# Two tags for the raw pieces at the changes of operands, and another order of PSUM banks in the plain groups of a gated MLP

## The chip, the cores and the metric

One core of a Trainium2 chip runs the whole kernel. The metric is the device time of one execution in microseconds; a kernel's time is the median of its runs. The engines are named as in the profile: PE (TensorE), ACT (ScalarE), DVE (VectorE), POOL (GpSimd) and SP (SyncE), whose instruction queue issues every DMA of this kernel.

## The reference

One decoder layer over 2048 tokens of width 1024: a mixer of three head groups with an output projection, then a gated MLP with a causal width-3 convolution on its gate branch, then a last norm. The change touches only the MLP's second half; the mixer is left out here.

```python
h = rmsnorm(x, norm_ffn[l])                                  # (2048, 1024)
gate = causal_dwconv(h @ ffn_w_gate[l], ffn_conv_w[l], ffn_conv_b[l])   # (2048, 2688)
x = x + (jax.nn.gelu(gate) * (h @ ffn_w_val[l])) @ ffn_w_down[l]        # 2688 -> 1024
...
return rmsnorm(x, norm_final)
```

## The kernel before

Matrix products run in a split float format: each operand is kept as a high and a low part (`split`, line 110: ACT copies the high part, DVE subtracts it from the raw tile for the low one), and each product takes three matmuls (`mm3`, line 134; the loop at line 1067). The large products of the MLP are 2x2 block products computed with seven block products in place of eight (`seven`, line 1062); the moving operand of such a product is held as four sets of tiles, `b1`, `t12`, `t34` and `b22` (`new_H`, line 895), which are the blocks and their sums. One `seven` is 84 matmuls of 128x512 and accumulates in one PSUM bank of tag `mm` (four banks), one of `sc` (two) and one of `aux` (two), asked for in that order.

The MLP is seven stages, in program order (lines 1251 to 1279):

- `up(0)`, for tokens 0 to 1023: 21 blocks `f` of 128 columns of the gate and value weights, one `seven` each. Its products are written to DRAM (`gx_d`, `gr_d`). Beside it `h_next` writes the operand tiles of the second token half, raw, to `hb_d`.
- `plain([(0, 4)])`: the first 5 of the 21 rows of `w_down` (NX = 5) as ordinary products, for 4 token tiles. Beside it `h_load` reads the raw operand pieces from `hb_d` and splits them into the operand tiles of `up(1)`: 14 pieces of 128x1024, three after each `f`.
- `up(1)`: tokens 1024 to 2047.
- `plain([(4, 4), (8, 2)])`: 4 and then 2 token tiles. Beside it `d_steps(0, H)` makes the operand tiles of `down(0)` out of 8 rows of `w_down`: four steps of two raw tiles of 128x1024, one after each of the first four `f`.
- `down(0)`: 8 rows of `w_down` for all tokens, 8 pairs of token tiles, one `seven` each.
- `plain([(10, 3), (13, 3)])`, beside it `d_steps(1, H)`; then `down(1)`, which also takes the last norm and writes the output.

These three `plain` stages are the changes of operands: while PE works through plain products, ACT and DVE make the next set of operand tiles. Below they are called the first, second and third change.

In `plain` (line 1146) each `f` loads a raw row of `w_down` (`load_w`, tag `wr` of pool `wraw`, three buffers; its parts `wh` and `wl` have three buffers, pool `wsp`) and a piece `graw` of the products (two buffers), splits both, and multiplies for every token tile `t` and both column halves `h`. The last two `f` are held back and run at the end, tile by tile; then ACT copies the two banks of `t` into a tile `y` (pool `op`, four buffers), which is stored to `ps_d`. With `n` token tiles one `f` is 6n matmuls.

What the raw tiles share:

- `wr`, three buffers: the raw weights of `plain` (`load_w`), those of `d_steps` (line 1002), and the raw weights of the stage that follows (`a_steps`, line 1031).
- `xt` of pool `xpool`, two buffers: the 14 pieces of `h_load` (line 991), and the sums `s12` and `s34` that `a_steps` makes for each `seven` (lines 1047 and 1053).
- `y`, four buffers in each change: the copied banks (line 1176), and in `down` the tiles that take the sums (line 1195). Its pool is opened where the tiles `gr`, `ga` and `v` of the `up` stage before were, so in the first and second change a `y` is free once those tiles of the last block are.

The banks of a group before:

```python
banks = [[aux_bank(), sc_bank()] if t < 2 else [mm_bank(), mm_bank()] for t in range(n)]
```

Each engine runs its own queue in order. The order within a queue is laid out when the kernel is built, by a planner that takes instructions by program order and by the offsets of `tc.high_priority`, and that gives out buffers as it expects them to come free; the splits of `plain` stand under such offsets (320 for the weights, 160 for `graw`), the copies of the banks do not.

Of the kernel before, what the change touches and what calls it, by code (L numbers as in the profile page):

```python
# [44 lines left out]
def kernel(ctx: ExitStack, tc: tile.TileContext, x, norm_mix, w_in, hgrn_lower_bounds, hgrn_norm,  # L45
# [669 lines left out]
    with ExitStack() as cy:  # L715
# [271 lines left out]

        def h_load(H):

            def piece(nm, k0):  # L990
                r = xpool.tile([P, D], F32, name="hr", tag="xt").rearrange("p (a b) -> p a b", b=TB)
                sync.dma_start(out=r, in_=hb_d[nm][:, k0:k0 + 2, :])
                put(r, H[nm], k0)
            return [lambda nm=nm, k0=k0: piece(nm, k0) for nm, n in (("t12", KT), ("b1", KT), ("b22", KH), ("t34", KT))
                    for k0 in range(0, n, 2)]

        def d_steps(r, H):

            def pair(k):
                raws = []  # L1000
                for f in (NX + KT * r + k, NX + KT * r + KH + k):
                    raws.append(wraw.tile([P, D], F32, name="wr", tag="wr"))
                    sync.dma_start(out=raws[-1], in_=w_down[f * P:(f + 1) * P, :])
# [142 lines left out]
        def plain(groups, gp, op, beside=()):  # L1146
# [3 lines left out]
            for t0, n in groups:  # L1150
                hf, at = t0 * P // TH, t0 * P % TH
                banks = [[aux_bank(), sc_bank()] if t < 2 else [mm_bank(), mm_bank()] for t in range(n)]
                ops = []
# [21 lines left out]
                for t in range(n):  # L1175
                    y = op.tile([P, D], F32, name="y", bufs=4)
                    for h in range(2):
                        for f in range(NX - 2, NX):
                            mms(t, h, f)
                        copy(act, y[:, h * 512:(h + 1) * 512], banks[t][h])  # L1180
                    sync.dma_start(out=ps_d[0][t0 + t], in_=y)
                    have[t0 + t].append(ps_d[0][t0 + t])

        def down(r, H, pairs, gp, op):
# [7 lines left out]
            def use(t0, W, steps):  # L1192
                ys = []
                for t in (t0, t0 + 1):
                    y = op.tile([P, D], F32, name="y", bufs=4)
                    sync.dma_start(out=y, in_=have[t][0])
# [63 lines left out]
        with ExitStack() as cu:  # L1260
            gp = pool_at(cu, 320, "f_g", 1, reuse_waits="tile")
            op = cu.enter_context(tc.tile_pool(name="f_o", bufs=1, reuse_waits="tile"))
            H = new_H()
            plain([(0, 4)], gp, op, h_load(H))
        with ExitStack() as cu:
# [3 lines left out]
        with ExitStack() as cu:  # L1269
            gp = pool_at(cu, 320, "f_g2", 1, reuse_waits="tile")  # L1270
            op = cu.enter_context(tc.tile_pool(name="f_o2", bufs=1, reuse_waits="tile"))
            H = new_H()
            plain([(4, 4), (8, 2)], gp, op, d_steps(0, H))
            nfb = xpool.tile([P, D], F32, name="nfb", tag="wbc", bufs=1)
            sync.dma_start(out=nfb, in_=norm_final.partition_broadcast(P))
            down(0, H, [10, 12, 14, 0, 2, 4, 6, 8], gp, op)
            H = new_H()
            plain([(10, 3), (13, 3)], gp, op, d_steps(1, H))
            down(1, H, [0, 2, 4, 6, 8, 10, 12, 14], gp, op)
# [30 lines left out]
```

## Time and profile before

| | us |
|---|---|
| median of 3 runs | 2254.43 |
| lowest and highest run | 2249.42, 2262.86 |
| the profiled execution | 2247.57 |
| its span, first to last instruction | 2245.8 |
| its time outside the span | 1.77 |

The profile is of one execution. Read it from the engine that is busiest, PE, and look for the stretches in which PE is not busy or runs at a lower granted clock; what ended the idle time is named behind the arrow of a row. A matmul's own duration in the trace is longer than the distance between the starts of two matmuls, since they are pipelined; the distance is what counts. In this document a stage's time is taken between the first matmul of the stage and the first one of the next.

### The profile page before, as it was taken

How to read it: one execution, taken by the hardware profiler on the slowest of the kernel's cores; microseconds unless marked ns; L12 is line 12 of the kernel's file. 1: busy time of each engine (PE TensorE's matmuls, PEld its weight loads, DVE VectorE, ACT ScalarE, POOL GpSimd, SP SyncE). 2: the span in 40 equal slices, each digit the busy share in tenths (PEclk: the TensorE clock that was granted, in tenths of full speed). 3: DMA queues.
4: the chain of work that ended last, by engine and by line, in shares of the span. 5: the costliest groups of instructions: out<-in, count | busy, mean ns of one | idle time of the engine just before them, and what ended most of it. 6: DMA issues, size and time to landing. Idle time of an engine off the chain costs nothing.

```text
span 2245.8 us, 31437 instructions
## 1 busy us (share of the span) xinstructions
PE 2153.5 (96%) x12118; PEld 1768.0 (79%) x12118; DVE 1679.3 (75%) x2366; ACT 990.4 (44%) x1361; POOL 353.6 (16%) x456
## 2 busy tenths in 40 slices
PE   7999999999999999999999999899999989998998
PEld 6887777777667788988888888788888867886886
DVE  7799998989678778777676766666666685777676
ACT  3443534432166276544444445444444463125332
POOL 2231332416243321000000000000000000000000
PEclk9999999999999999999999999999999999998999
DMA  7453422346145645644233337422222248646653
GB/s 261 123 165 93 154 83 64 91 159 198 38 136 207 186 152 177 205 129 129 88 123 99 125 100 231 130 85 85 85 85 85 85 166 279 223 169 223 216 181 112
DMA packets 313699, 321.41 MB, mean 143 GB/s; under 512 B 17347, under 2 KB 267214, under 8 KB 312014
## 3 DMA queue, kind: packets, MB, share of 16 engines
q1 hardware_dynamic: 313550, 319.41, 43.9%
q8 instruction: 95, 1.56, 0.3%
q14 instruction: 54, 0.44, 0.1%
HBM read 233.38 MB, written 85.98 MB: 142 GB/s over the span
## 4 chain that ended last, share of the span: by engine, by line
PE 51%; DVE 8%; DMA 6%; ACT 3%; issue 2%; POOL 0%; SPq 0%; DVEq 0%; POOLq 0%; ACTq 0%
PE mm L1068 26%; PE sc L1068 13%; PE aux L1068 6%; DMA wr<-in_ffn_w_down_dram 1%; PE sc L137 1%; DVE wl L113 1%; PE sc L136 1%; PE sc L138 1%; DMA xt<-x_d 1%; DMA y<-ps_d 1%; DMA x_d<-xr 1%; DMA hr<-hb_t 1%; ACT wh L106 1%; PE mm L913 1%; DVE xc L801 1%
## 5 line engine op out<-in xcount | busy, mean ns | idle before, releaser
L106 ACT ACTIVATE wh<-wr 128x1024 fp32r<-128x1024 f32 (+3 forms) x217 | 201.1, 929 | 362.8 <-PE aux L1068 85.0
L113 DVE TENSOR_TENSOR wl<-wr,wh 128x1024 fp32r<-128x1024 f32 (+2 forms) x241 | 261.2, 1086 | 114.8 <-ACT wh L106 110.4
L106 ACT ACTIVATE wh<-s 128x1024 fp32r<-128x1024 f32 x116 | 123.0, 1061 | 253.4 <-PE sc L1068 197.2
L138 PE MATMUL mm<-hTh,wl 128*128 128x512 f32 x576 | 230.5, 400 | 2.8 <-POOL wl L113 2.3
L136 PE MATMUL mm<-hTh,wh 128*128 128x512 f32 x576 | 232.9, 405 | 0.0
L137 PE MATMUL mm<-hTl,wh 128*128 128x512 f32 x576 | 231.0, 401 | 0.0
L404 POOL TENSOR_TENSOR qc<-Q,X 32x128 f32<-32x128 f32 x224 | 151.1, 675 | 247.1 <-ACT X L390 116.4
L1068 PE MATMUL mm<-t34h,wh 128*128 128x512 f32 x464 | 181.0, 390 | 1.1 <-DVE y L1233 0.9
L1068 PE MATMUL mm<-t34h,wl 128*128 128x512 f32 x464 | 180.6, 389 | 0.0
L1068 PE MATMUL mm<-t34l,wh 128*128 128x512 f32 x464 | 180.6, 389 | 0.0
L113 DVE TENSOR_TENSOR wl<-s,wh 128x1024 fp32r<-128x1024 f32 x116 | 141.5, 1221 | 15.0 <-ACT wh L106 14.8
L137 PE MATMUL sc<-wl,oh 128*128 128x256 f32 x512 | 147.8, 289 | 2.2 <-DVE wl L113 2.2
L136 PE MATMUL sc<-wh,oh 128*128 128x256 f32 x512 | 147.5, 289 | 2.1 <-DVE xr L834 2.1
L138 PE MATMUL sc<-wh,ol 128*128 128x256 f32 x512 | 146.3, 286 | 0.0
L138 PEld LDWEIGHTS mm<-hTh,wl 128*128 128x128 f32 x576 | 108.2, 188 | 31.3 <-issue 4.3
L136 PEld LDWEIGHTS mm<-hTh,wh 128*128 128x128 f32 x576 | 108.1, 188 | 28.8 <-issue 7.1
L137 PEld LDWEIGHTS mm<-hTl,wh 128*128 128x128 f32 x576 | 108.2, 188 | 27.8 <-issue 7.3
L1137 DVE SCALAR_TENSOR_TENSOR ga<-gr,pcol,ga 128x1024 f32<-128x1024 f32 x84 | 107.6, 1281 | 0.6 <-issue 0.3
L1068 PEld LDWEIGHTS mm<-t34h,wh 128*128 128x128 f32 x464 | 87.1, 188 | 21.2 <-issue 1.7
L137 PEld LDWEIGHTS sc<-wl,oh 128*128 128x128 f32 x512 | 98.4, 192 | 5.9 <-issue 2.9
L136 PEld LDWEIGHTS sc<-wh,oh 128*128 128x128 f32 x512 | 98.1, 192 | 5.1 <-DVE xr L834 2.7
L1068 PEld LDWEIGHTS mm<-t34h,wl 128*128 128x128 f32 x464 | 87.1, 188 | 18.2
(331 smaller groups left out, 5520.3 us busy)
## 6 DMA issues: line engine op xcount, KB each, us to landing
wr<-in_w_in_dram SPq DMA_DIRECT2D x80, 512.0 KB
wr<-in_ffn_w_gate_dram SPq DMA_DIRECT2D x42, 512.0 KB
wr<-in_ffn_w_val_dram SPq DMA_DIRECT2D x42, 512.0 KB
wr<-in_ffn_w_down_dram SPq DMA_DIRECT2D x41, 512.0 KB
wr<-in_w_out_dram SPq DMA_DIRECT2D x32, 512.0 KB
gr_d<-v SPq DMA_DIRECT2D x32, 512.0 KB
ps_d<-y SPq DMA_DIRECT2D x32, 512.0 KB
wr<-gr_d SPq DMA_DIRECT2D x32, 512.0 KB
```

What stands on the lines that cost most here:

```text
L106: act.activation(o, i, AF.Copy)
L113: e_lo.tensor_tensor(lo, raw, hi.bitcast(F32), op=ALU.subtract)
L136: pe.matmul(o, lh, rh, start=first, stop=False)
L137: pe.matmul(o, lh, rl, start=False, stop=False)
L138: pe.matmul(o, ll, rh, start=False, stop=last)
L404: pool.tensor_tensor(qc[p_, h, :].rearrange("p (n s) -> p n s", s=lev), qo[p_, 2], xo[p_, 2], op=ALU.mult)
L801: vec.tensor_tensor_scan(xc[:, i, :], r[:, i, :], th[:, i, :], initial=hs0[:, c:c + 1], op0=ALU.mult, op1=ALU.add)
L913: pe.transpose(out=pt[:, k * P:(k + 1) * P], in_=xt[:, (k0 + k) * P:(k0 + k + 1) * P], identity=ident)
L1068: pe.matmul(o, lhs[a], rhs[b], start=first and k == 0 and i == 0, stop=last and k == KH - 1 and i == 2, skip_group_check=True)
L1137: vec.scalar_tensor_tensor(ga, gr[:, k:k + TH], pc[f"fw{k}"][:, f:f + 1], ga, op0=ALU.mult, op1=ALU.add)
```

## The change

- A function `spare(op)` gives a tile of tag `y` (four buffers) or, without a pool, of tag `xt` (two buffers).
- `h_load`: the pieces of `b22` and `t34` (6 of 14) go through `y`, the others stay in `xt`.
- `d_steps`: the raw weights of steps 1 and 3 go through `y`, those of steps 0 and 2 through `xt`; none goes through `wr` any more.
- `plain`: token tile 0 and 1 take two banks of `mm` each, tile 2 the two of `sc`, tile 3 the two of `aux`; before it was `aux` and `sc` for tiles 0 and 1, `mm` for 2 and 3. The copies of the banks get a priority offset of 120.
- The tiles `y` of `plain` and `down` are the same ones as before, now written `spare(op)`.

No instruction of arithmetic and no transfer is added or taken away.

```diff
@@ -985,21 +985,25 @@
                 keep(T["t1"], "t34", KH, t)
             return [lambda f=f, t=t: f(t) for t in range(NTK) for f in (s_norm, s_a, s_b, s_c, s_d)]
 
-        def h_load(H):
+        def spare(op):
+            return op.tile([P, D], F32, name="y", tag="y", bufs=4) if op else \
+                xpool.tile([P, D], F32, name="hr", tag="xt")
+
+        def h_load(H, op):
 
             def piece(nm, k0):
-                r = xpool.tile([P, D], F32, name="hr", tag="xt").rearrange("p (a b) -> p a b", b=TB)
+                r = spare(op if nm in ("b22", "t34") else None).rearrange("p (a b) -> p a b", b=TB)
                 sync.dma_start(out=r, in_=hb_d[nm][:, k0:k0 + 2, :])
                 put(r, H[nm], k0)
             return [lambda nm=nm, k0=k0: piece(nm, k0) for nm, n in (("t12", KT), ("b1", KT), ("b22", KH), ("t34", KT))
                     for k0 in range(0, n, 2)]
 
-        def d_steps(r, H):
+        def d_steps(r, H, op):
 
             def pair(k):
                 raws = []
                 for f in (NX + KT * r + k, NX + KT * r + KH + k):
-                    raws.append(wraw.tile([P, D], F32, name="wr", tag="wr"))
+                    raws.append(spare(op if k % 2 else None))
                     sync.dma_start(out=raws[-1], in_=w_down[f * P:(f + 1) * P, :])
                 (b11, b12), (b21, b22) = [(a[:, :TB], a[:, TB:]) for a in raws]
 
@@ -1149,7 +1153,7 @@
             every = -(-len(beside) // nst)
             for t0, n in groups:
                 hf, at = t0 * P // TH, t0 * P % TH
-                banks = [[aux_bank(), sc_bank()] if t < 2 else [mm_bank(), mm_bank()] for t in range(n)]
+                banks = [[mk() for _ in range(2)] for mk in (mm_bank, mm_bank, sc_bank, aux_bank)[:n]]
                 ops = []
 
                 def mms(t, h, f):
@@ -1173,11 +1177,12 @@
                         st_()
                     cnt += 1
                 for t in range(n):
-                    y = op.tile([P, D], F32, name="y", bufs=4)
+                    y = spare(op)
                     for h in range(2):
                         for f in range(NX - 2, NX):
                             mms(t, h, f)
-                        copy(act, y[:, h * 512:(h + 1) * 512], banks[t][h])
+                        with tc.high_priority(offset=120):
+                            copy(act, y[:, h * 512:(h + 1) * 512], banks[t][h])
                     sync.dma_start(out=ps_d[0][t0 + t], in_=y)
                     have[t0 + t].append(ps_d[0][t0 + t])
 
@@ -1192,7 +1197,7 @@
             def use(t0, W, steps):
                 ys = []
                 for t in (t0, t0 + 1):
-                    y = op.tile([P, D], F32, name="y", bufs=4)
+                    y = spare(op)
                     sync.dma_start(out=y, in_=have[t][0])
                     ys.append(y)
                     for src in have[t][1:]:
@@ -1261,7 +1266,7 @@
             gp = pool_at(cu, 320, "f_g", 1, reuse_waits="tile")
             op = cu.enter_context(tc.tile_pool(name="f_o", bufs=1, reuse_waits="tile"))
             H = new_H()
-            plain([(0, 4)], gp, op, h_load(H))
+            plain([(0, 4)], gp, op, h_load(H, op))
         with ExitStack() as cu:
             upools = [pool_at(cu, 8192, "f_up1", 1, reuse_waits="tile")]
             upools.insert(0, cu.enter_context(tc.tile_pool(name="f_up0", bufs=1, reuse_waits="tile")))
@@ -1270,12 +1275,12 @@
             gp = pool_at(cu, 320, "f_g2", 1, reuse_waits="tile")
             op = cu.enter_context(tc.tile_pool(name="f_o2", bufs=1, reuse_waits="tile"))
             H = new_H()
-            plain([(4, 4), (8, 2)], gp, op, d_steps(0, H))
+            plain([(4, 4), (8, 2)], gp, op, d_steps(0, H, op))
             nfb = xpool.tile([P, D], F32, name="nfb", tag="wbc", bufs=1)
             sync.dma_start(out=nfb, in_=norm_final.partition_broadcast(P))
             down(0, H, [10, 12, 14, 0, 2, 4, 6, 8], gp, op)
             H = new_H()
-            plain([(10, 3), (13, 3)], gp, op, d_steps(1, H))
+            plain([(10, 3), (13, 3)], gp, op, d_steps(1, H, op))
             down(1, H, [0, 2, 4, 6, 8, 10, 12, 14], gp, op)
```

## Rows read from the trace of the kernel before

**Rows 1.** Page: busy time, share of the span and instructions of each engine.

```profile
PE 2153.5 (96%) x12118; PEld 1768.0 (79%) x12118; DVE 1679.3 (75%) x2366; ACT 990.4 (44%) x1361; POOL 353.6 (16%) x456
```

**Rows 2.** Windows: length, busy PE PEld DVE ACT POOL, PEclk, DMA share, GB/s.

```profile
1437.00:1817.00 380.00, 380.00 (x1678) 314.67 (x1677) 248.25 (x284) 165.81 (x206) 25.67 (x39) 1.00 0.27 86
...
1840.00:1860.00 20.00, 16.21 (x59) 12.59 (x58) 13.85 (x21) 14.07 (x23) 0.00 (x0) 0.83 0.66 241
1860.00:1880.00 20.00, 18.91 (x80) 14.51 (x80) 11.21 (x13) 8.26 (x12) 0.00 (x0) 1.00 0.93 309
2040.00:2060.00 20.00, 13.02 (x32) 9.49 (x33) 15.12 (x24) 11.26 (x19) 0.00 (x0) 0.66 0.52 169
```

**Rows 3.** Timeline of PE: start, duration, line, out<-in, idle before it.

```profile
1380.43 0.39 PE L136 MATMUL aux<-wh,gh 128*128 128x512 f32 x1
...
1436.54 0.39 PE L1068 MATMUL mm<-hTh,wh 128*128 128x512 f32 x1
...
1817.34 0.39 PE L136 MATMUL aux<-wh,gh 128*128 128x512 f32 x1
...
1838.86 0.50 PE L136 MATMUL aux<-wh,gh 128*128 128x512 f32 x1 [3.17 <-ACT wh L106]
...
1848.38 0.79 PE L136 MATMUL aux<-wh,gh 128*128 128x512 f32 x1 [3.79 <-ACT wh L106]
...
1871.98 0.39 PE L1068 MATMUL mm<-hTh,wh 128*128 128x512 f32 x1
...
2024.90 0.39 PE L136 MATMUL aux<-wh,gh 128*128 128x512 f32 x1
...
2081.64 0.39 PE L1068 MATMUL mm<-hTh,wh 128*128 128x512 f32 x1
```

**Rows 4.** Waits around the three changes in turn: total us, times, longest.

```profile
PE sc L1068 <- ACT wh L106: 3.9, 1, 3.9
...
PE mm L1068 <- ACT y L106: 1.9, 1, 1.9
...
PE aux L136 <- ACT wh L106: 9.3, 4, 3.8
...
PE aux L136 <- ACT wh L106: 7.7, 3, 3.9
...
PE mm L1068 <- DVE y L1229: 0.7, 1, 0.7
```

**Rows 5.** Chain that ended last, around the three changes: start, us, what.

```profile
1413.33 5.57 DMA hr<-hb_t
...
1833.32 4.41 DMA wr<-in_ffn_w_down_dram
...
2080.55 6.04 DMA y<-ps_d
```

**Rows 6.** Timeline of DVE in the first and the second change.

```profile
1416.80 1.23 DVE L113 TENSOR_TENSOR t34l<-hr,t34h 128x1024 fp32r<-128x1024 f32 x1 [3.50 <-ACT t34h L106]
1418.06 0.69 DVE L1048 TENSOR_TENSOR s<-wr 128x512 f32<-128x512 f32 x1
...
1822.30 1.22 DVE L1140 TENSOR_TENSOR v<-ga,v 128x1024 f32<-128x1024 f32 x1
...
1850.18 0.69 DVE L1021 TENSOR_TENSOR st<-wr,st 128x512 f32<-128x512 f32 x1
```

**Rows 7.** SP's own waits, third change: total us, times, longest.

```profile
SPq L1003 <- DVE st L1018: 9.0, 3, 3.2
...
SPq L122 <- DVE wl L113: 7.5, 3, 3.7
```

**Rows 8.** Windows over the second change, its first group, and the third change.

```profile
1807.00:1872.00 65.00, 55.63 (x228) 43.78 (x227) 51.23 (x73) 40.77 (x65) 2.25 (x1) 0.95 0.65 225
1807.00:1853.00 46.00, 37.55 (x154) 29.58 (x153) 42.22 (x62) 28.99 (x48) 2.25 (x1) 0.94 0.56 191
2014.00:2082.00 68.00, 58.92 (x231) 46.18 (x230) 49.32 (x71) 38.16 (x59) 0.00 (x0) 0.90 0.66 218
```

## The prediction

> **What bounds the kernel now.** I read the busy times first: PE is busy 96% of the span, no other engine above 79% [rows 1]. So a change that removes no arithmetic can only give back what PE loses, and the next question is where that is. The table of busy times by stretch answers it. In the long stretch of `up(1)` PE never rests: 1678 matmuls in 380.0 us, 0.2265 us from start to start, at a clock of 1.00 [rows 2]. In the stretches around the changes of operands it rests, and the granted clock falls as far as 0.83 and 0.66 on a mean over 20 us [rows 2]. [...] The fall stands behind idle times of PE in each case.
>
> The loss of each change is its length between first matmuls [rows 3] less its matmuls, counted from the code, at 0.2265 us:
> - first change with the first `seven` behind it: 1380.43 to 1436.54, 56.1 us; 5 x 24 + 84 = 204 matmuls, 46.2 us; lost 9.9.
> - second: 1817.34 to 1871.98, 54.6 us; 5 x 24 + 5 x 12 = 180, 40.8 us; lost 13.9.
> - third: 2024.90 to 2081.64, 56.7 us; 2 x 5 x 18 = 180, 40.8 us; lost 16.0, and 0.7 more just behind it, where `down(1)` waits for its first sum [rows 4].
>
> Together 40.5 us, clock losses included. What PE waited for is named by the waits and the chain. First change: 1.9 us for a bank that ACT had not yet copied, 3.9 us for the high part of `s12` [rows 4]; on the chain stand the pieces `hr`, 5.6 us each, one behind another, and `s12` itself begins right when a piece frees its `xt` buffer [rows 5, 6]. Second and third: 9.3 and 7.7 us for the high part of a plain weight [rows 4], which waited for its load, 4.4 us from issue to landing [rows 5]; two steps begin 9.5 us apart, where 24 matmuls take 5.4 [rows 3]. SP's waits say why: the loads of `d_steps` (L1003) and of `plain` (L122) both stand waiting for DVE to finish with an earlier raw tile [rows 7]. Three `wr` buffers serve three raw tiles a step.
>
> **The change part by part.** *Pieces through `y`.* 6 of the 14 pieces leave `xt`; the other 8 end with `b1`. `s12` then waits only for those, so it is made some 20 us earlier (8 pieces ahead of it, not 14, in a chain of about 60 us), and the 3.9 us with its clock loss goes. What is late next is the buffer for its parts: `wh` has three, and the two last `f` hold two of them to the end of the group. PE then has 12 matmuls of the first product, 2.7 us, in which the low part's subtraction takes 1.23 us [rows 6] and the copy before it may take as long. `down(0)` at 1871.98 begins in the same pattern, and no idle time stands before it [rows 3]. Bounds: 0 to 3.9. The `t34` pieces are needed only 48 matmuls, 10.9 us, after the start of `up(1)`.
>
> *Banks.* In the first change the first bank asked for next (`mm`) was that of tile 2; now it is tile 0's, copied 36 held-back matmuls (8 us) before the end. The 1.9 us goes. In the second change the group of two now ends on all four `mm` banks, and `down(0)` asks for one at once; tile 0's was finished 18 matmuls, 4.1 us, before, and the whole wait for such a copy is 1.9 us now [rows 4]. Nothing, unless the copy is late (rival below). I put the first change at 1.0 left of 9.9, nearer the zero end because its causes are both taken away: **8.9**.
>
> *Raw weights out of `wr`.* `plain` has the three `wr` buffers to itself and can load three rows ahead; the raw tiles of the steps have two `xt` and four `y` buffers. In the second change the first `y` buffers are free when the last `up` block has been multiplied (1822.3 to 1823.5) [rows 6], early enough for step 1. The waits for `wh` have no cause left in the loads. What is late next is DVE: it is busy 51.2 of the 65 us of the second change and 49.3 of the 68 us of the third [rows 8]. With 13.9 and 16.0 us taken out, 51.1 and 52.0 remain, so DVE would be busy nearly without a break. Over the 46 us in which the second change's steps are made its packing is 42.2 of 46, 0.918 [rows 8]. At that packing it needs 55.8 and 53.7 us: 4.7 and 1.7 too many. Of the four steps' work, four subtractions of 0.69 [rows 6] (for the `t34` parts of the last one) may come 10.9 us into `down`, which takes off some 2. Bounds 0 and 4.7; I take 2.5 and 1.7.
>
> *DMA.* The second change moves 225 GB/s over 65 us, 14.6 MB, the third 218 over 68, 14.8 MB [rows 8]. The busiest 20 us moved 309 GB/s at a share of 0.93 [rows 2]; at that rate 47.3 and 48.0 us, inside the 51.1 and 52.0 that would remain, but with little to spare. It is tight at the end of the second change, where a step of 12 matmuls lasts 2.7 us and bank stores and the loads of `down(0)` meet. If the 6.2 MB of that busiest row had all to land within the 13.6 us of the group of two, 20 - 13.6 = 6.4 us would be lost; if the earlier loads have cleared the way, nothing more than today's 0.9. I take 3.0. In the third, `y` tiles for `down(1)` took 6.0 us to land [rows 5]; I leave 1.3 for them, between 0 and 3.
> [...]
>
> Second change: 13.9 - 2.5 - 3.0 = **8.4**. Third: 16.7 - 1.7 - 1.3 = **13.7**. Sum 8.9 + 8.4 + 13.7 = 31.0 us. The profiled execution took 2247.6 us (span 2245.8, 1.8 outside), so it would be 2216.6; the median of the runs shown is 6.9 us above that execution, and from it I forecast 2254.4 - 31.0 = 2223.4 us.
>
> **The rivals.**
> - *DVE and ACT take the steps first.* With all raw tiles there early, the four steps' splits (over half of what DVE does in a change) could be laid out ahead of the plain weights; a step would stay at 9.5 us, only its releaser being another. For it: DVE at 42 of 46 us already. Against it: the plain splits stand under a priority offset of 320, the steps' under none. Gain 8.9 and some 2.5 of the second groups: 2243 us.
> - *The copies wait for raw tiles.* Copies and steps now share four `y`. The copy of tile 2 needs the buffer of step 3's first raw tile, which DVE last read at 1850.2 [rows 6]; without stalls, tile 2 is complete at 1817.3 + 27.2 - 2.7 = 1841.8. ACT would stand up to 8.4 us, with the splits of the next group behind it; 2.7 us of those are covered by the `f` already split. That is 5.7 us in the second change and about as much, 6.7, in the third, where tile 2's `sc` banks are also asked for again: 31 - 12.4 = 18.6 us, 2236 us. Against it: a planner that sees the buffer taken will put ready work first. [...]
> - *The transfers set the pace anyway.* If DMA and not the buffers is behind the 5.6 us of a piece, earlier issues land no earlier: 2254 us, no change. For it: a share of 0.93 at 1860 to 1880. Against it: only 0.66 and 0.52 in the 20 us that hold the worst stalls [rows 2].
> - *Slower: SP stands in front of a raw tile.* Place: the first groups of the second and third change. If the loads of steps 1 to 3 are queued ahead of the plain loads, SP stands until their `y` or `xt` buffer is free, and the plain loads behind it start only then. A step would then last a step's DVE work, 7 to 8 us (42.2 us for four steps, five plain splits and the tail of `up`), and then a load of 4.4 and its split, 1.2 [rows 5, 6]: 12.6 to 13.6 us in place of 9.5, so some 3.5 us lost in each of eight steps, 28, against 8.9 gained in the first change: about 2273 us. It decides from a step of 9.5 + 8.9/8 = 10.6 us. For it: SP already spends 9.0 and 7.5 us at L1003 and L122 in the third change [rows 7]. Against it: six more buffers stand free for these tiles than `wr` had.
>
> **How the numbers follow.** Chances: forecast 0.62; steps first 0.16; copies wait 0.09; transfers 0.06; slower 0.07. A measurement of this kernel can tell about 0.5% from no change, 11.3 us. The forecast and the copies rival are faster by more; steps first lies at the bound, so half of it counts as faster: faster 0.79, same 0.08 + 0.06 = 0.14, slower 0.07. Range: if no loss at all is left, 2254.4 - 40.5 = 2213.9, and less the spread of the runs below the median, 5.0, about 2210. Upwards it takes in steps first and its spread, 2248. Left out are transfers and slower, 0.13, and the tails.
>
> **What would show it.** In the profile after: starts of two steps of the first groups 5.4 to 6 us apart, no wait of PE for a `wh` above 1 us, clock 1.00 from 1360 to the end of the third change; `s12` made before the last plain matmul of the first change; `wr` filled by lines 122 and 1032 alone; DVE over 9.5 tenths busy in the first groups. The forecast is wrong if steps still begin 9 us apart with another releaser (DVE, then ACT standing at a `y`), if SP's wait at the raw loads grows, or if the loads land 6 us and more after their issue.

## The result and the profile after

| | before | after |
|---|---|---|
| median of 6 runs each, us | 2253.05 | 2223.19 |
| lowest and highest, us | 2249.42, 2262.86 | 2215.95, 2227.22 |
| the profiled execution, us | 2247.57 | 2215.95 |
| its span, us | 2245.8 | 2214.2 |

The ratio of the runs is 0.9859, with a 95% interval of 0.9832 to 0.9886: faster by 1.1 to 1.7%. The changed kernel was timed once more later, beside an experiment: 2216.54 us against 2255.37 for the kernel before, a ratio of 0.9838 (0.9812 to 0.9864). The forecast was 2223.4 us.

The busy times, from the page of the kernel after (answers [rows 1]): PE's busy time is 10.8 us shorter and its idle time 20.8 us shorter (2245.8 - 2153.5 = 92.3 before, 2214.2 - 2142.7 = 71.5 now). The work is the same, 12118 matmuls, so the busy time that went is, as far as it belongs to the change, busy time per matmul: over the second and the third change [rows 8] PE was busy 0.244 and 0.255 us for each at a clock of 0.95 and 0.90, and is now, in the last two windows below, 0.230 and 0.228 at 1.00. Between two profiles of the changed kernel it differs by 2.6 us (2142.7 and 2145.3).

```profile
PE 2142.7 (97%) x12118; PEld 1761.8 (80%) x12118; DVE 1678.8 (76%) x2366; ACT 987.5 (45%) x1361; POOL 349.3 (16%) x456
```

Windows of the kernel after (length, busy PE PEld DVE ACT POOL, PEclk, DMA share, GB/s); the first three answer [rows 2], the last two, over the second and the third change, [rows 8]:

```profile
1840.00:1860.00 20.00, 18.58 (x78) 14.07 (x77) 18.59 (x26) 14.63 (x24) 0.00 (x0) 1.00 0.84 277
1860.00:1880.00 20.00, 20.00 (x89) 16.54 (x89) 12.66 (x18) 3.82 (x4) 0.00 (x0) 1.00 0.80 281
2040.00:2060.00 20.00, 20.00 (x90) 16.51 (x89) 13.03 (x19) 8.58 (x13) 0.00 (x0) 1.00 0.84 293
...
1802.00:1859.00 57.00, 55.58 (x242) 44.70 (x241) 52.19 (x74) 42.11 (x68) 0.19 (x1) 1.00 0.78 266
1998.00:2053.00 55.00, 54.72 (x240) 44.71 (x239) 49.46 (x73) 38.38 (x61) 0.00 (x0) 1.00 0.76 254
```

The clock of 0.83 and 0.66 in the second and third change is 1.00 in this profile (a second profile of the changed kernel has 0.91 from 1840 to 1860, see the last section), and the transfers run at 266 and 254 GB/s, before at 225 and 218.

Timeline of PE of the kernel after (start, duration, line, out<-in, idle before it), the starts that answer [rows 3] and the waits of the first two changes:

```profile
1377.51 0.39 PE L136 MATMUL mm<-wh,gh 128*128 128x512 f32 x1
1381.74 0.50 PE L136 MATMUL mm<-wh,gh 128*128 128x512 f32 x1 [1.80 <-ACT v L1139]
...
1408.40 0.39 PE L1072 MATMUL mm<-hTh,wh 128*128 128x512 f32 x1
1413.23 0.50 PE L1072 MATMUL sc<-t12h,wh 128*128 128x512 f32 x1 [1.95 <-ACT wh L106]
...
1812.27 0.39 PE L136 MATMUL mm<-wh,gh 128*128 128x512 f32 x1
...
1817.71 0.39 PE L136 MATMUL mm<-wh,gh 128*128 128x512 f32 x1
...
1823.15 0.39 PE L136 MATMUL mm<-wh,gh 128*128 128x512 f32 x1
...
1844.03 0.50 PE L137 MATMUL mm<-wl,gh 128*128 128x512 f32 x1 [1.13 <-DVE wl L113]
...
1855.72 0.39 PE L1072 MATMUL mm<-hTh,wh 128*128 128x512 f32 x1
...
2009.11 0.39 PE L136 MATMUL mm<-wh,gh 128*128 128x512 f32 x1
...
2050.77 0.39 PE L1072 MATMUL mm<-hTh,wh 128*128 128x512 f32 x1
```

Steps of the second change begin 5.44 us apart, which is 24 matmuls with nothing lost, where two of them stood 9.5 us apart before. The plain matmuls of the second change take 43.5 us (1812.27 to 1855.72) in place of 54.6, of the third 41.7 in place of 56.7; 40.8 is the time without a loss. The first change goes the other way: its plain matmuls take 30.9 us, before 29.3, and PE waits twice, once at its start and once in the first `seven`.

For the comparison of all kernels I cut each trace at the first matmul of each change. "First" is the first change with `up(1)`, "second" the second with `down(0)`, "third" the third to the last matmul, "sum" the three together; "start wait" is PE's wait for the fourth `mm` bank, at the eleventh matmul of the first change, "entry wait" that for the parts of `s12` (high and low together where both are late). All in us, from one profile each.

| kernel | before it | first | second | third | sum | start wait | entry wait |
|---|---|---|---|---|---|---|---|
| before | 1380.4 | 436.9 | 207.6 | 212.4 | 856.9 | none | 3.92 |
| after | 1377.5 | 434.8 | 196.8 | 196.6 | 828.2 | 1.80 | 1.95 |
| after_again | 1383.2 | 431.3 | 199.9 | 197.1 | 828.3 | 1.38 | 1.75 |
| raws_only | 1382.3 | 437.1 | 197.9 | 197.0 | 832.1 | none | 5.00 |
| banks_only | 1386.2 | 437.6 | 209.2 | 209.1 | 855.9 | 1.89 | 5.22 |
| pieces_only | 1384.5 | 431.0 | 207.4 | 212.0 | 850.4 | none | 0.50 |
| four_last_mm | 1379.8 | 431.8 | 199.4 | 196.3 | 827.5 | none | 2.57 |
| no_prio | 1378.5 | 433.6 | 196.9 | 197.2 | 827.7 | 2.23 | 1.43 |
| all_xt | 1379.7 | 431.9 | 199.6 | 198.1 | 829.6 | 1.89 | 1.83 |
| first_mmlast_noprio | 1382.7 | 431.8 | 196.0 | 196.2 | 824.0 | none | 2.18 |
| first_noprio_t34 | 1380.0 | 431.7 | 196.8 | 195.6 | 824.0 | none | 2.61 |
| s12_first | 1379.9 | 430.0 | 197.4 | 196.4 | 823.8 | 1.21 | 0.53 |
| first_s12 | 1381.5 | 432.1 | 196.9 | 197.1 | 826.1 | none | 2.22 |
| s12_start | 1385.2 | 430.4 | 199.4 | 195.2 | 824.9 | none | 1.96 |

The column "before it" is work that the change leaves alone: up to that matmul the instructions of each engine stand in the same order in the profiles of the kernels before and after (8530 matmuls, 1588 instructions of DVE, 876 of ACT, 398 of POOL). The two profiles of the changed kernel differ there by 5.7 us, and the kernel before lies between them. So of the 31.6 us between the two spans 2.9 belong to the executions and 28.7 to the change. The rows of after and after_again also say how far one profile's stage can be trusted: 3.5 us in the first, 3.1 in the second, 0.5 in the third. Differences below that between two rows of the table prove nothing by themselves; a wait that is there in every kernel with one edit and in none without does.

### The profile page after: what moved, and what is told of

The parts are those of the page before. It is cut to its first block, busy times and chain, and to the rows that moved or that the text cites. A ratio compares the mean times of both kernels' runs of the same rounds, so it can differ in the third digit from the quotient of the medians.

```text
span 2214.2 us, 31440 instructions
## 1 busy us (share of the span) xinstructions
PE 2142.7 (97%) x12118; PEld 1761.8 (80%) x12118; DVE 1678.8 (76%) x2366; ACT 987.5 (45%) x1361; POOL 349.3 (16%) x456
## 4 chain that ended last, share of the span: by engine, by line
PE 54%; DVE 7%; DMA 5%; ACT 2%; issue 2%; POOL 0%; SPq 0%; DVEq 0%; POOLq 0%; ACTq 0%
PE mm L1072 26%; PE sc L1072 13%; PE aux L1072 6%; PE sc L137 2%; PE sc L138 2%; PE sc L136 2%; DVE wl L113 1%; DMA x_d<-xr 1%; PE mm L138 1%; PE mm L136 1%; PE mm L137 1%; DMA xt<-x_d 1%; DVE xc L801 1%; DMA y<-ps_d 1%; PE mm L913 1%
## 5 line engine op out<-in xcount | busy, mean ns | idle before, releaser
L1072 PEld LDWEIGHTS mm<-t34l,wh 128*128 128x128 f32 x464 | 87.1, 188 | 17.9
```

What stands on the lines that cost most here:

```text
L1072: pe.matmul(o, lhs[a], rhs[b], start=first and k == 0 and i == 0, stop=last and k == KH - 1 and i == 2, skip_group_check=True)
```

## The experiments

My theory after the result: the raw weights taken out of `wr` give nearly the whole gain; the pieces through `y` give some in the first change; the new order of banks gives nothing and makes the start wait. The rivals: that the banks and the offset on their copies carry the gain, that it needs the four buffers of `y` and not just an empty `wr`, and, for what is left in the first change, the different causes that the last groups of runs take apart.

**One part alone: raw weights.** The kernel before with `spare` and

```diff
-                    raws.append(wraw.tile([P, D], F32, name="wr", tag="wr"))
+                    raws.append(spare(op if k % 2 else None))
```

> The kernel before with one part of the change: the raw weights of the steps of the second and third change go through xt and y, not through wr; banks, copies and the pieces of the first change stay as before. Theory (the plain loads waited for wr buffers): nearly all of what the second and third change gained, 10.7 and 15.8 us in the traces before and after, so 25 to 27 us less than before, about 2227 us; steps of the first groups 5.5 to 6 us apart; first change as before with its waits of 1.9 and 3.9 us. Rival (the order of the banks and the earlier copies carry half of it or more): 13 us less at most, 2240 us, with PE waiting for banks in the second and third change.

Measured: 2225.29 us against 2253.53, ratio 0.9882 (0.9858 to 0.9905). Second and third stage are as short as in the changed kernel, the first as long as before. The waits of its first change (PE, what it waited for: total us, times, longest) are those of [rows 4], a little longer:

```profile
PE sc L1072 <- ACT wh L106: 5.0, 1, 5.0
PE mm L1072 <- ACT y L106: 2.0, 1, 2.0
```

So this part alone is worth 24.8 us of stage sum (856.9 - 832.1) of the change's 28.7.

**One part alone: banks and copies.** The kernel before with the new list of banks and the offset of 120 on the copies.

```diff
-                banks = [[aux_bank(), sc_bank()] if t < 2 else [mm_bank(), mm_bank()] for t in range(n)]
+                banks = [[mk() for _ in range(2)] for mk in (mm_bank, mm_bank, sc_bank, aux_bank)[:n]]
```

> The kernel before with one part of the change: only the order of the banks and the priority of the copies. Theory: steps of the second and third change stay 9 to 9.5 us apart, the waits for wh stay (9.3 and 7.7 us); in the first change the wait of 1.9 us for a bank at its end goes and one of about 1.8 us with a stretch at the lower clock comes at its start; in all within 4 us of before. Rival (banks carry the gain): 10 us or more less than before.

Measured: 2251.34 us, ratio 0.9993 (0.9977 to 1.0009). No change. Its waits, first in the second and then in the first change:

```profile
PE mm L136 <- ACT wh L106: 9.2, 4, 3.8
...
PE mm L136 <- ACT v L1135: 1.9, 1, 1.9
```

The 9.3 us of [rows 4] for the high part of a plain weight stand there unchanged, only under another bank's name, and the start wait is there. That it comes from this part is shown: six rows of the table (five kernels, one of them profiled twice) ask for all four `mm` banks at the start of the first change, and these six have the wait; the other eight have none.

**One part alone: pieces.** The kernel before with `b22` and `t34` through `y`.

```diff
-                r = xpool.tile([P, D], F32, name="hr", tag="xt").rearrange("p (a b) -> p a b", b=TB)
+                r = spare(op if nm in ("b22", "t34") else None).rearrange("p (a b) -> p a b", b=TB)
```

> The kernel before with one part of the change: only the six pieces b22 and t34 of the first change go through y. Theory from the trace after: s12 is made early, but its high part stands on ACT behind copies that wait for a y still held by a piece, so half of the 3.9 us remains and the wait for a bank at the end of the group (1.9 us) stays or grows; 0 to 5 us less than before, all in the first change. Rival (as forecast, both waits gone): about 8 us less, 2245 us. Second and third change as before.

Measured: 2245.42 us, ratio 0.9968 (0.9951 to 0.9984). Second and third stage as before, the first 5.9 us shorter. Its waits of the first change:

```profile
PE mm L1072 <- ACT y L106: 2.3, 1, 2.3
PE sc L1072 <- DVE wl L113: 0.5, 1, 0.5
```

The wait for `s12` has gone from 3.92 to 0.50; the bank wait in front of it, which the new banks were to take away, is still there, and it hides part of what `s12` still needs. So each of the two expectations was half right: the wait for `s12` went as in the rival, the bank wait stayed as in the theory, and the gain, 8.1 us by the medians, is the rival's and not the 0 to 5 that I expected. The three parts alone give 24.8 + 1.0 + 6.5 = 32.3 us by stage sums, the change 28.7; the 3.6 us between are about what two profiles of one kernel differ by in the first stage. No run has the raw weights and the pieces without the banks.

**The tag of the raw weights.** The changed kernel with all raw weights of `d_steps` in the two buffers of `xt`.

```diff
-                    raws.append(spare(op if k % 2 else None))
+                    raws.append(spare(None))
```

> The changed kernel with the raw weights of all four steps of the second and third change in xt (two buffers), none in y. Theory (the freed wr gives the plain loads their way, but the steps need a second pair of buffers so that a load lies under the DVE work of the step before): PE never waits for a plain load, but each step waits for its load of 4 to 5 us, 12 to 14 us of DVE idle per change, so the operand tiles come late and down starts late: 5 to 9 us more in each of the second and third change, 2233 to 2241 us. Rival (only the freed wr counts): within 3 us of the changed kernel, 2223 to 2226 us.

Measured: 2220.91 us against 2250.39, ratio 0.9863 (0.9844 to 0.9881). The second stage, 199.6, is inside what the changed kernel's own two profiles show; the third is 1.0 to 1.5 longer. So two spare buffers give most of what six do: what counts most is that `wr` is left to the plain weights. They do not give quite all: the changed kernel without the offset of the copies (no_prio, below) took 2216.66 us in the same set of runs, 4.3 us less, and none of its four runs is as long as the shortest here; in the third stage PE waits 1.87 us for the first sum of `down(1)`. My expectation that without the second tag 5 to 9 us go in each stage fell. No run leaves all raw weights in `wr` and gives that tag more buffers, so whether the tag of their own or the mere number of buffers did it stays open.

**Four tiles: `mm` last for one of them.** The changed kernel with the four-tile groups in another order of banks.

```diff
-                banks = [[mk() for _ in range(2)] for mk in (mm_bank, mm_bank, sc_bank, aux_bank)[:n]]
+                kinds = (mm_bank, sc_bank, aux_bank, mm_bank) if n == 4 else (mm_bank, mm_bank, sc_bank)[:n]
+                banks = [[mk() for _ in range(2)] for mk in kinds]
```

> The changed kernel with the banks of a group of four tiles in the order mm, sc, aux, mm in place of mm, mm, sc, aux. Theory: the 1.8 us wait at the start of the first change is for the mm bank that the last product of up(0) still holds until ACT copies it; asked for 12 matmuls later it is free, and the wait and the stretch at the lower clock behind it go: the first change's plain group 27.2 to 27.6 us in place of 30.9, about 3.5 us less than the changed kernel, 2220 us. Rival (ACT is late whatever the order, and the next bank is waited for in the same way): within 1 us of the changed kernel.

Measured: 2217.60 us, ratio 0.9854 (0.9826 to 0.9881). The start wait is gone, the first plain group takes 27.2 us, its 120 matmuls without a loss. In the second change the group of two then asks for `mm` banks that were used last, and PE waits 1.0 us for one of them, the second row:

```profile
PE mm L136 <- ACT wh L106: 1.8, 1, 1.8
PE mm L136 <- ACT y L106: 1.0, 1, 1.0
```

The wait for `wh` is not shown to come from the order (the changed kernel's second profile has one of 1.14 us there), and the second stage, 199.4, lies between the changed kernel's two.

**The offset of the copies.** The changed kernel without it.

```diff
-                        with tc.high_priority(offset=120):
-                            copy(act, y[:, h * 512:(h + 1) * 512], banks[t][h])
+                        copy(act, y[:, h * 512:(h + 1) * 512], banks[t][h])
```

> The changed kernel without the priority offset of 120 of the copies of the banks. Theory: in the first change the offset puts copies that wait for a y ahead of the high part of s12 on ACT; without it the wait of 1.95 us at the second product of up(1) falls below 1 and the first change with up(1) is 1 to 3 us shorter than the changed kernel's 434.8; second (196.8) and third change (196.6) within 1 us: about 2221 us. Rival (the second and third change need the copies early): 2 to 6 us more in these two.

Measured: 2216.66 us, ratio 0.9843 (0.9825 to 0.9861). The wait for the high part fell below 1 as expected, to 0.90, but one of 0.53 for the low part came behind it. The first two stages lie between the changed kernel's two profiles, the third is 0.1 to 0.6 longer. The offset brings nothing that these runs can show.

**Both in the first change only.** The changed kernel, first group alone: banks `mm, sc, aux, mm` and no offset; then the same with only `t34` through `y`.

```diff
-                banks = [[mk() for _ in range(2)] for mk in (mm_bank, mm_bank, sc_bank, aux_bank)[:n]]
+                kinds = (mm_bank, mm_bank, sc_bank, aux_bank) if t0 else (mm_bank, sc_bank, aux_bank, mm_bank)
+                banks = [[mk() for _ in range(2)] for mk in kinds[:n]]
...
-                        with tc.high_priority(offset=120):
+                        with tc.high_priority(offset=120 if t0 else 0):
```

> The changed kernel with two edits in the first change only: banks in the order mm, sc, aux, mm, and no priority offset for the copies; the later changes as in the changed kernel. Theory (the two causes by which the first change gave 2 us and not 8.9): plain group 27.2 us in place of 30.9, wait at the second product of up(1) below 1 us, first change with up(1) 428 to 430.5 us in place of 434.8; second and third change as in the changed kernel, 196.8 and 196.6; about 5 us less than the changed kernel, 2218 us. Rival (the t34 loads hold ACT and y whatever the order): the 1.95 us stay, 432 us.

Measured: 2216.69 us, ratio 0.9851 (0.9826 to 0.9876).

```diff
-                r = spare(op if nm in ("b22", "t34") else None).rearrange("p (a b) -> p a b", b=TB)
+                r = spare(op if nm == "t34" else None).rearrange("p (a b) -> p a b", b=TB)
```

> As the kernel with mm, sc, aux, mm and no offset in the first change, and besides the two b22 pieces back in xt, so that each t34 piece has a y of its own and no piece waits for one. Theory (what counts is that s12 need not wait for t34; a second pass through y costs nothing once the copies stand behind): first change with up(1) within 1 us of that kernel. Rival (the t34 pieces, loaded late in a second pass, are what is late): 1 to 3 us less. Third possibility (s12 waits for b22): 2 to 4 us more.

Measured: 2215.08 us, ratio 0.9851 (0.9820 to 0.9882). In both the start wait is gone and the entry wait stays, 2.2 and 2.6 us. Neither the offset nor the buffers of the `b22` pieces is its cause.

**What the entry waits for.** ACT's timeline of the kernel after, at the start and at the end of the first change:

```profile
1377.09 1.06 ACT L106 ACTIVATE t12h<-hr 128x1024 fp32r<-128x1024 f32 x1 [1.04 <-DMA hr<-hb_t]
1378.06 1.23 ACT L1136 ACTIVATE ga<-gr,pcol 128x1024 f32<-128x1024 f32 x1
1379.19 1.04 ACT L106 ACTIVATE wh<-wr 128x1024 fp32r<-128x1024 f32 x1
1380.57 0.63 ACT L106 ACTIVATE gh<-graw 128x512 fp32r<-128x512 f32 x1 [0.34 <-DMA graw<-gx_d]
1381.10 0.58 ACT L1139 ACTIVATE v<-mm 128x512 f32<-128x512 f32 x1
...
1409.23 1.06 ACT L106 ACTIVATE t34h<-y 128x1024 fp32r<-128x1024 f32 x1 [0.73 <-DMA y<-hb_t]
1410.20 1.07 ACT L106 ACTIVATE y<-sc 128x512 f32<-128x512 f32 x2
1411.15 1.08 ACT L106 ACTIVATE y<-aux 128x512 f32<-128x512 f32 x2
1412.11 2.02 ACT L106 ACTIVATE wh<-s 128x1024 fp32r<-128x1024 f32 x2
```

The last row is the high part of `s12`. It could not begin before the third `wh` buffer was free, at the last plain matmuls (the `seven` begins at 1408.40), but it begins 3.7 us after that, behind a `t34` piece that had to land and behind four copies. To tell buffer and order apart, an offset puts that one split ahead of three of the copies:

```diff
-                W["y"] = parts(W["s12"])
+                with tc.high_priority(offset=ahead):
+                    W["y"] = parts(W["s12"])
...
+            return a_steps(..., 320 if hf and f == 0 else 0)
```

> The changed kernel, with a priority offset of 320 on the split of the first s12 of up(1) alone: on ACT its high part comes ahead of three copies of the last banks instead of behind them; two t34 pieces still stand before it. If the copies in front of it are the cause of the wait of 1.95 us at the entry of up(1) in the changed kernel, that wait falls by about 1.5 us to 0.4 and the first change with up(1) from 434.8 to about 433 us, or 432 if the half clock behind the wait goes too. If the cause is the free wh buffer (the third one comes free with the last matmuls of the group), or the transfer that the t34 piece before it waits for, the wait stays above 1.5 us and the stage at 434 to 435. The rest as in the changed kernel: second change with down(0) 197, third 197; total 2219 to 2223.

Measured: 2214.32 us against 2252.05, ratio 0.9835 (0.9811 to 0.9858). ACT's timeline, and under it PE's only wait at the entry:

```profile
1408.92 1.06 ACT L106 ACTIVATE t34h<-y 128x1024 fp32r<-128x1024 f32 x1 [0.19 <-DMA y<-hb_t]
1410.09 0.60 ACT L106 ACTIVATE y<-sc 128x512 f32<-128x512 f32 x1
1410.58 1.05 ACT L106 ACTIVATE wh<-s 128x1024 fp32r<-128x1024 f32 x1
1411.53 0.59 ACT L106 ACTIVATE y<-sc 128x512 f32<-128x512 f32 x1
```

```profile
1412.94 0.50 PE L1073 MATMUL sc<-t12h,wl 128*128 128x512 f32 x1 [0.53 <-DVE wl L113]
```

The split begins 1.9 us after the `seven` in place of 3.7, and the wait for the high part is gone. The buffer comes free early enough; the cause is what stands ahead on ACT. Of the 1.8 us some 0.6 are the `t34` split before it, which begins 0.3 us after the `seven` in place of 0.8, and the rest the three copies. In the second profile of the changed kernel ACT stands only 0.15 us for a transfer there, in place of 0.73, and PE waits 1.75 us all the same.

**The same in the other variants.** The offset on `s12` together with the two edits of the first group, and together with the order of banks alone:

> The changed kernel with the two first-change edits of an earlier run (banks of the first group in the order mm, sc, aux, mm, no offset for its copies) and the offset of 320 on the split of the first s12. Here the offset moves the high part ahead of one bank copy only, and a t34 piece that comes late by DMA still stands before it. Copies theory: 0.5 us less than the 1.65 us wait of that run, first change with up(1) 431.3. Buffer theory: 431.8 as without the offset. If the t34 piece alone sets it, no change either. Total 2214 to 2218.

Measured: 2216.67 us, ratio 0.9843 (0.9824 to 0.9862); entry wait 2.22. Here the offset moves the split ahead of one copy only, and a `t34` split that stood 2.19 us for its transfer puts off everything behind it. The half microsecond that I expected of one copy less did not show.

> The changed kernel with two edits in the first change: the offset of 320 on the split of the first s12, which puts it ahead of the last three bank copies on ACT, and the banks of the first group in the order mm, sc, aux, mm (the offset of 120 on the copies stays). If the two causes are independent, the start wait of 1.8 us and the entry wait both go, plain takes 27.2 to 28 us and the first change with up(1) 428 to 429, against 434.8 in the changed kernel, so that with the other stages as there the time is some 6 us below the changed kernel of the same batch. If the mm banks asked for last are copied too late for up(1), or the t34 piece that waits for its transfer comes first again, the entry wait stays near 1.5 us with its half clock: 431 to 432, some 3 us below.

> The changed kernel once more, without an edit, beside the run before it on the same chip. The stages as in its first profile if they belong to the kernel: first change with up(1) 434 to 436, second with down(0) 196 to 198, third 196 to 198; a wait at the entry of up(1) near 2 us, and one of about 1.8 at its start. What stands before the first change may differ by some 9 us, as it did among the kernels that share it.

Measured side by side, s12_start and after_again: 2220.12 (2214.26 to 2222.24) and 2216.54 us (2216.01 to 2221.82), both at a ratio of 0.9838. The start wait is gone in s12_start, the entry wait is 1.43 + 0.53: there the `t34` split ahead of `s12` waits 0.91 us for its transfer. Its stage sum is 3.4 us shorter, which its runs do not show: its median lies 3.6 us above. In the second profile of the changed kernel the first stage is 431.3, where I expected 434 to 436, the second 199.9, where I expected 196 to 198, and the third as expected. So no version is shown to be faster than the changed kernel; s12_first has the lowest median and the lowest stage sum (823.8), but its interval overlaps with that of the changed kernel.

## Why the prediction was right, and where it was not

The waits of PE in the kernel after, around the first, second and third change, in the order of [rows 4]:

```profile
PE sc L1072 <- ACT wh L106: 1.9, 1, 1.9
PE mm L136 <- ACT v L1139: 1.8, 1, 1.8
...
PE mm L137 <- DVE wl L113: 1.1, 1, 1.1
PE mm L1072 <- DVE y L1234: 0.7, 1, 0.7
...
PE sc L136 <- ACT y L106: 0.3, 1, 0.3
```

The total is right, the split is not: forecast 8.9 + 8.4 + 13.7 = 31.0; by stages the first profile of the changed kernel has 2.2 + 10.7 + 15.8 = 28.7, the second 5.6 + 7.6 + 15.3 = 28.5. The medians differ by 29.9 us in one set of runs and by 38.8 in the other, so that the forecast of 2223.4 beside 2223.19 is closer than the measurement can tell: an error of 3 to 7 us in the first change stood against errors of 2 us the other way in the third and, in one of the two profiles, in the second. That they cancel is luck; the range, 2210 to 2248, did not need it.

- *Raw weights out of `wr`: right, and for the reason given.* 9.3 and 7.7 us of waits for `wh` [rows 4] are gone, with the clock loss behind them, and raws_only alone shows it. Steps are 5.44 us apart, as "what would show it" asked; its other signs came less well: the clock is 0.83 twice in the first change, and the second profile keeps one wait of 1.14 us for a `wh`.
- *What is late next is DVE: right in kind.* In the second change PE waits 1.13 us for a `wl` that DVE makes. I left 2.5 + 3.0 = 5.5 us there; 43.5 - 40.8 = 2.7 were left (4.4 in the second profile). In the third I left 3.0; 0.9 were left (0.4 in the second profile, and its 0.7 in `down(1)`). DVE got by because it began earlier, not because it packed better: its packing is 52.2 of 57 us, 0.916, against the 0.918 that I had assumed, but with the raw tiles in `xt` both loads of the first step are issued by 1797; before, the first one was at 1792.5 and the second at 1807.9. The sum that needs both stands 12.3 us ahead of the first plain matmul (1812.27), before 2.8 us ahead of it (1817.34). DVE after, and then before:

```profile
1799.93 0.69 DVE L1018 TENSOR_TENSOR st<-hr,st 128x512 f32<-128x512 f32 x1 [1.61 <-DMA hr<-in_ffn_w_down_dram]
```

```profile
1814.55 0.69 DVE L1014 TENSOR_TENSOR st<-wr,st 128x512 f32<-128x512 f32 x1
```

- *DMA, 3.0 and 1.3: mis-sized.* What is left of it is the 0.7 us for `y` in `down(0)`, behind loads of 6.4 and 7.0 us with DVE's work between and after them; in the second profile it is 0.5 us in `down(0)`, behind a load of 5.1, and 0.7 in `down(1)`, behind one of 6.6, while a wait of 1.1 us in `down(0)` has no load on its chain. Transfers of the kernel after from 1800 to 1860, sum and slices of 1.5 us:

```profile
GB/s 214 335 153 202 105 203 341 262 332 321 371 309 123 270 46 366 339 306 382 391 385 57 63 221 375 417 63 317 72 67 175 363 351 346 323 313 395 315 320 322
DMA packets 8099, 15.95 MB, mean 266 GB/s; under 512 B 599, under 2 KB 4311, under 8 KB 8094
```

  I had taken 309 GB/s for the busiest 20 us and so for the most that can be moved. It is the busiest of the windows of [rows 2], not of the trace: this one, early in the kernel before, moved 381.

```profile
30.00:50.00 20.00, 20.00 (x99) 16.61 (x100) 17.17 (x63) 4.51 (x6) 0.00 (x0) 1.00 1.03 381
```

  At that rate, as an estimate from its bytes, the 14.6 MB of the second change take 38.3 us in place of my 47.3, well inside the 51.1, and next to nothing is left for this term; the 0.7 and 0.5 us that were left in `down(0)` agree better with that than with my 3.0. Single slices of 1.5 us above reach 371 to 417 GB/s.
- *First change, 1.0 left of 9.9: the step that failed.* 8.1 were left in the first profile (434.8 less 1884 matmuls at 0.2265 us, 426.7) and 4.6 in the second, where the same sum gives 10.2 before. The part on the pieces held as far as it went: the sums for `s12` begin at 1394.9, 13.5 us before the `seven`, as this timeline of DVE shows against the 1418.06 of [rows 6]:

```profile
1394.86 0.69 DVE L1052 TENSOR_TENSOR s<-wr 128x512 f32<-128x512 f32 x1
```

  But I then looked only for the buffer of the parts and took `down(0)`, where no piece and no late copy stands on ACT, as the model. What was late next was ACT's queue: `t34` pieces and bank copies in front of the split. s12_first shows it in one profile. The bounds of that wait, 0 to 3.9, held it (1.95); my choice near zero did not, and for a clock loss behind it and for the start wait the sum had no term.
- *Banks: "the 1.9 us goes" was right, its price was overlooked.* I followed the banks to the end of the group, where the new order helps, and not to its start, where it asks for a bank that the last product of `up(0)` has filled and ACT has not copied yet. The copy of that bank is the row at 1381.10 above. Four instructions stand ahead of it from 1377.09 on; the first had waited 1.04 us for its piece, the last waits 0.34 us for its transfer, and PE stands 1.80 us. In the six profiles with this wait the copy begins 3.0 to 4.0 us after the first plain matmul, and the wait goes with it, 1.21 to 2.23 us; the 0.34 us stand in this one alone. By the part alone, the runs show no gain: 0.9993.

The rival of the copies rests on ACT holding everything behind an instruction that is not ready. The row at 1380.57 shows that once: ACT stands 0.34 us for a transfer, while the copy behind it, whose last matmul ended at 1377.67, is not taken ahead.

The rivals: *DVE and ACT take the steps first* fell with the 5.44 us between steps. *The transfers set the pace* fell with 266 GB/s. *The copies wait for raw tiles* fell where I had placed it: in the kernel after PE has no wait for a copy above 0.3 us in the second and third change. Yet its mechanism, ACT held by one instruction that is not ready, is part of what acts in the first. *Slower: SP stands in front of a raw tile* fell too. SP's waits of the third change: one of the kernel before that stands beside [rows 7], and then those after, which answer them:

```profile
SPq L1003 <- DVE wl L113: 10.0, 3, 8.0
```

```profile
SPq L122 <- DVE wl L113: 14.7, 7, 6.2
...
SPq L1007 <- DMA ps_d<-y: 1.8, 1, 1.8
```

With all that ended them, the waits at the plain loads grew from 9.7 to 14.7 us, and cost nothing: the loads that they hold back are not missed, for PE waits for no `wh` in that change any more. Those at the raw tiles of `d_steps` fell from 19.3 (10.0 + 9.0 + 0.3) to 2.0 us in these windows (2014 to 2082 and 1998 to 2053), and from 20.8 to 5.4 counted from 25 us ahead of the change. So SP's wait at the raw loads, my sign against the forecast, came out both ways, and the other sign, loads that land 6 us and more after their issue, came with the 6.4 and 7.0 us above and did not decide either. A longer wait of a queue or a late landing counts only where an engine misses what it holds back.

## What to carry to other kernels

When two streams of tiles with different times of life share one tag, look first at giving the stream that is needed soon the tag for itself; how many buffers the other gets mattered far less here. When a buffer or bank is given back earlier at one end of a stage, follow the same resource to the other end, where somebody now asks for it earlier. And once a wait on a buffer is gone, list what stands ahead of the next instruction on its engine's queue, pieces that wait for a transfer among it, before calling the remainder zero.

## What the runs showed of the hardware

The same kernel had nearly the same waits at the first change in two profiles, and the granted clock fell behind them in one alone. Windows of the kernel after, then of after_again (the start wait is 1.80 and 1.38 us, the entry wait 1.95 and 1.75), and then of all_xt, where the start wait is 1.89:

```profile
1380.00:1390.00 10.00, 8.26 (x29) 6.68 (x30) 7.90 (x9) 6.58 (x9) 0.00 (x0) 0.83 0.86 298
1410.00:1420.00 10.00, 8.05 (x29) 6.03 (x28) 6.08 (x7) 5.32 (x9) 1.43 (x2) 0.83 0.51 177
```

```profile
1380.00:1390.00 10.00, 8.62 (x38) 6.70 (x37) 9.34 (x10) 7.76 (x9) 1.04 (x1) 1.00 0.89 307
1410.00:1420.00 10.00, 8.19 (x36) 6.12 (x35) 6.50 (x8) 7.87 (x12) 0.78 (x2) 1.00 0.90 328
...
1840.00:1860.00 20.00, 17.73 (x71) 14.02 (x70) 18.78 (x29) 14.04 (x24) 0.00 (x0) 0.91 0.81 271
```

```profile
1380.00:1390.00 10.00, 8.11 (x36) 6.40 (x35) 9.10 (x10) 8.40 (x10) 0.08 (x1) 1.00 0.91 303
```

The clock of 0.83 is a mean over ten microseconds: in slices of one it is 0.50 from 1384 to 1386 and from 1414 to 1417, and 1.00 from 1387 to 1413. Eight distances between matmul starts, from 1383.00 and from 1413.85, take 3.38 and 3.37 us there, 0.42 us each, where at 0.2265 they would take 1.81; some 1.6 us are put off, twice, which is most of the 3.5 us by which the first stage of the two profiles differs (434.8 and 431.3). In the second change it was the other way round: after_again waits 1.14 and 1.13 us there and its clock is 0.91, while the first profile, with one wait of 1.13, stays at 1.00. The length of a wait alone does not tell, for all_xt waits longer than after_again at the start and, at the entry, 1.83 us, as long as it, and its clock does not fall there either (from 1415.38 on its matmul starts stand 0.22 to 0.24 us apart). Why the clock fell in the one and not in the other stays open. And work whose instructions and order are the same reached the first change between 1377.5 and 1383.2 us in two executions of one kernel, so that stage lengths, not times from the start, are to be compared.
